# Seven block products for eight contraction tiles in two output projections

## The chip, the cores and the metric

The kernel runs on one core of a Trainium2 chip. Its time is the device time of one execution in microseconds (us). A core has five engines that run their own instruction lists and wait for each other by semaphores: TensorE (PE in the profile; PEld is its weight load), VectorE (DVE), ScalarE (ACT), GpSimd (POOL) and SyncE (SP), which here issues DMA transfers. Matmuls write into PSUM, a small memory of eight banks; all else lies in SBUF.

## The reference

The program is a trunk of two layers on a sequence of T = 512 tokens and D = 1024 channels in float32. Each layer has a sequence mixer (a state-space mixer in the first, a spatial gating mixer in the second) and a channel mixer, each followed by a layer norm of `sqrt(2) * x + y`. The channel mixer is what the change touches:

```
def conv_ffn(x, w_in, conv_w, conv_b, w_out):      # x: 512 x 1024
    h = causal_dwconv(x @ w_in, conv_w, conv_b)    # 512 x 5632, 3 taps along the tokens
    g, u = split(h, 2)                             # 512 x 2816 each
    return (silu(g) * u) @ w_out                   # (512 x 2816) @ (2816 x 1024)
...
x = layer_norm(sqrt(2) * x + conv_ffn(x, ...))
```

The contraction of the output projection has 2816 = 22 x 128 channels, so 22 tiles.

## The kernel before

*Split float32.* A product of two float32 matrices is done as three products of rounded parts. Each operand `a` is split into `hi` (a cast by ACT to the matmul's float32 format) and `lo = a - hi` (a subtraction by DVE), and PE adds up `hi*hi + hi*lo + lo*hi` in one PSUM bank. So each 128x128 by 128x512 block costs three matmuls.

*Weights.* All weights lie in DRAM as a list of 250 tiles of 128x1024 (`wall`). `w_prep` (lines 74 to 84) goes through that list: SP loads a tile into one of three raw buffers (L78), ACT casts it (L80), DVE subtracts (L82). `hi` and `lo` have seven buffers each, and `w_get(i)` has tiles up to i + 6 prepared before it hands out tile i.

*Channel mixer.* `ffn` (from line 542) runs 22 steps; step j multiplies two weight tiles with the layer's transposed input (`xT_hi`, `xT_lo`: 8 x 512 columns each, kept in split form), convolves both results on ACT and DVE (L178, L180) and stores `silu(gate) * up` as `h[:, j, :]`, 128 channels by 512 tokens (L565). In step 1 `affine_res` applies the last norm's scale and bias to the residual `xres` (L309, L310).

*Output projection.* `out_proj` (from line 205) takes all eight PSUM banks as an accumulator `acc[t][h]`: four row blocks of 128 tokens by two halves of 512 columns. For each contraction tile k it gets the split activation tile (`Split.get`, L192 and L193, six buffers), the split weight tile, and does 4 x 2 x 3 = 24 matmuls (L214 to L216). The last four or five tiles are done row block by row block, so that `stats` (L252 on) can add the residual (L259), do the norm's statistics and scale while PE is at the next row block. POOL does `(var + eps) ** -0.5` there on 128x1 elements (L203).

*Order.* The program is written as tiles and operations in one text. A scheduler gives each engine its list from planned times and the order of the text; the lists are then run in order, and an instruction whose semaphore isn't there holds up all that stand behind it on its engine.

Of the kernel before, what the change touches and what calls it, by code (L numbers as in the profile page):

```python
# [14 lines left out]
P = 128  # L15
T = 512
# [33 lines left out]
LOOK = 6  # L50


@with_exitstack
def trunk_kernel(ctx, tc, x_tok, x_t, w_dt, wall, pp, ln_g, ln_b, b_v, b_s, w_s_t, out):
# [17 lines left out]
    wnext = [0]  # L72

    def w_prep(upto):
        while wnext[0] <= min(upto, W_ALL - 1):
            i = wnext[0]
            raw = wpool.tile([P, 1024], F32, tag="wraw", bufs=3, name=f"wraw{i}")
            nc.sync.dma_start(raw, wall[i])  # L78
            hi = wpool.tile([P, 1024], F32R, tag="whi", bufs=WB, name=f"whi{i}")
            nc.scalar.copy(hi, raw)  # L80
            lo = wpool.tile([P, 1024], F32R, tag="wlo", bufs=WB, name=f"wlo{i}")
            nc.vector.tensor_sub(lo, raw, hi.bitcast(F32))  # L82
            wready[i] = (hi, lo)
            wnext[0] += 1

    def w_get(i, look=LOOK):
        w_prep(i + look)
        return wready.pop(i)
# [3 lines left out]
    xT_hi = const.tile([P, NK, T], F32R, name="xT_hi")  # L92
    xT_lo = const.tile([P, NK, T], F32R, name="xT_lo")
# [29 lines left out]
    def mm_k(o, w, k, lo, hi):  # L123
        whi, wlo = w
        cs = slice(k * P, (k + 1) * P)
        nc.tensor.matmul(o, whi[:, cs], xT_hi[:, k, lo:hi], start=(k == 0), stop=False)  # L126
        nc.tensor.matmul(o, whi[:, cs], xT_lo[:, k, lo:hi], start=False, stop=False)  # L127
        nc.tensor.matmul(o, wlo[:, cs], xT_hi[:, k, lo:hi], start=False, stop=(k == NK - 1))  # L128

    with tc.tile_pool(name="xload", bufs=8) as xl:  # L130
        wdt = xl.tile([P, NK, 32], F32, name="wdt", bufs=1)
        xr = []
        for q in range(4):
            for k in (2 * q, 2 * q + 1):
                xr.append(xl.tile([P, T], F32, tag="xr", name=f"xr{k}"))
                nc.sync.dma_start(xr[k], x_t[:, k, :])
                nc.scalar.copy(xT_hi[:, k, :], xr[k])
                nc.vector.tensor_sub(xT_lo[:, k, :], xr[k], xT_hi[:, k, :].bitcast(F32))
# [44 lines left out]
    class Split:  # L183
# [4 lines left out]
        def pre(self, k, tag=""):  # L188
            bufs = self.bufs if not tag else 1
            hi = self.pl.tile([P, T], F32R, tag="ahi" + tag, bufs=bufs, name=f"ahi{self.base}_{k}")  # L190
            lo = self.pl.tile([P, T], F32R, tag="alo" + tag, bufs=bufs, name=f"alo{self.base}_{k}")
            nc.scalar.copy(hi, self.act(k))  # L192
            nc.vector.tensor_sub(lo, self.act(k), hi.bitcast(F32))  # L193
            self.done[k] = (hi, lo)
# [10 lines left out]
    def out_proj(lnp, split, base, nk, ln, last, hooks=None, nxt=None, mid=None):  # L205
        if last:
            gb, bb = ln_bc(lnp, base, ln)
        acc = [[pst(f"acc{base}_{t}_{h}") for h in range(2)] for t in range(NT)]

        def mm(t, h, k, a, w):  # L210
            o = acc[t][h]
            ts_ = slice(t * P, (t + 1) * P)
            hs = slice(h * T, (h + 1) * T)
            nc.tensor.matmul(o, a[0][:, ts_], w[0][:, hs], start=(k == 0), stop=False)  # L214
            nc.tensor.matmul(o, a[0][:, ts_], w[1][:, hs], start=False, stop=False)  # L215
            nc.tensor.matmul(o, a[1][:, ts_], w[0][:, hs], start=False, stop=(k == nk - 1))  # L216

        k0 = 0
        if hooks is not None:
# [32 lines left out]
        def stats(t):  # L252
            r = lnp.tile([P, D], F32, tag="r", bufs=2, name=f"r{base}_{t}")
# [21 lines left out]
        def trans(t):  # L275
            for h in range(2):
# [9 lines left out]
                xh = xT_hi[:, 4 * h:4 * h + 4, t * P:(t + 1) * P]  # L286
                nc.scalar.copy(xh, xf)
                nc.vector.tensor_sub(xT_lo[:, 4 * h:4 * h + 4, t * P:(t + 1) * P], xf, xh.bitcast(F32))
# [10 lines left out]
    def ln_bc(pl, base, ln):  # L299
        gb = pl.tile([P, D], F32, name=f"lng{base}")  # L300
        bb = pl.tile([P, D], F32, name=f"lnb{base}")
# [242 lines left out]
    def ffn(ip, base_o, li, ln, last, nxt=None):  # L544
        with ExitStack() as st:
# [3 lines left out]
            split = Split(sp, base_o, lambda k: h[:, k, :])  # L549
# [17 lines left out]
            out_proj(lnp, split, base_o, 22, ln, last, nxt=nxt)  # L567


    def v_tile(cb, t, ws):  # L570
        ps = pst(f"pv{cb}_{t}")
        ts_ = slice(t * P, (t + 1) * P)
        for k in range(NK):
            whi = ws[k // 2][0][:, (k % 2) * T:(k % 2) * T + T]
            wlo = ws[k // 2][1][:, (k % 2) * T:(k % 2) * T + T]
            nc.tensor.matmul(ps, xT_hi[:, k, ts_], whi, start=(k == 0), stop=False)  # L576
            nc.tensor.matmul(ps, xT_hi[:, k, ts_], wlo, start=False, stop=False)  # L577
            nc.tensor.matmul(ps, xT_lo[:, k, ts_], whi, start=False, stop=(k == NK - 1))  # L578
# [98 lines left out]
def _pack(i):  # L677
# [27 lines left out]
    wall = np.concatenate(tiles, 0)  # L705

# [54 lines left out]
```

## Time and profile before

| | us |
|---|---|
| median of 3 runs | 1439.64 |
| lowest, highest | 1439.13, 1439.78 |
| the profiled execution | 1439.39 |
| its span, first to last instruction | 1437.5 |
| PE busy | 1423.6 (99%) |
| DVE busy | 846.1 (59%) |
| ACT busy | 611.5 (43%) |
| POOL busy | 23.7 (2%) |

The profile is one execution. It has the busy time of each engine, the span in 40 equal slices with the clock that TensorE was granted, the chain of work that ended last, the costliest groups of instructions, and each instruction with its start. A matmul's listed duration overlaps that of the next; the distance of their starts is what each costs.

### The profile page before, as it was taken

Reading aid. Unit: us, or ns where it says so; the run is one execution under the profiler, and the core shown is the slowest. Engines: PE = TensorE matmul, PEld = TensorE weight load, DVE = VectorE, ACT = ScalarE, POOL = GpSimd, SP = SyncE. Lnnn points to the kernel's source line nnn. Section 1 sums busy time; section 2 is a strip of 40 time slices with the busy share of each in tenths; the row PEclk is TensorE's granted clock in tenths of the full one; section 3 lists DMA queues with packets and bytes.
Section 4 is the critical chain, followed back from the end, with each engine's and each line's share of the span. In section 5 each row is a group of like instructions: output and inputs, shape, how many; then the busy total and the mean of one; then the engine's idle time right before and its main releaser. Section 6 shows DMA issues by size and latency. Waiting matters only on the chain.

```text
span 1437.5 us, 17317 instructions
## 1 busy us (share of the span) xinstructions
PE 1423.6 (99%) x6911; PEld 1187.8 (83%) x6911; DVE 846.1 (59%) x1147; ACT 611.5 (43%) x893; POOL 23.7 (2%) x30
## 2 busy tenths in 40 slices
PE   8999999999999999999999999999999999999997
PEld 6788888888889888888888888888888888888886
DVE  6878777565378655554336556446378655554336
ACT  5886677343245433333233433223255433333220
POOL 0000000000000000000000000000000000000001
PEclk9999999999999999999999999999999999999999
DMA  6533322333424332323331432223223333333311
GB/s 219 206 106 129 106 100 74 88 115 122 160 73 123 112 99 92 103 90 101 93 98 59 154 125 88 88 88 118 89 81 127 101 103 93 98 103 118 103 44 59
DMA packets 42864, 152.66 MB, mean 106 GB/s; under 512 B 4760, under 2 KB 6040, under 8 KB 41504
## 3 DMA queue, kind: packets, MB, share of 16 engines
q1 hardware_dynamic: 40240, 143.17, 31.0%
q10 hardware_dynamic: 2544, 8.39, 1.7%
q8 instruction: 54, 0.88, 0.2%
q14 instruction: 26, 0.21, 0.0%
HBM read 149.37 MB, written 2.18 MB: 105 GB/s over the span
## 4 chain that ended last, share of the span: by engine, by line
PE 96%; ACT 1%; DVE 1%; DMA 1%; issue 0%; SPq 0%; DVEq 0%; ACTq 0%
PE ip L126 18%; PE ip L127 18%; PE ip L128 18%; PE acc L216 10%; PE acc L214 10%; PE acc L215 10%; PE pv L576 2%; PE pv L578 2%; PE pv L577 2%; PE psp L636 1%; PE py L443 1%; PE pt L279 1%; PE po L450 1%; PE pst L429 1%; PE pcb L384 0%; PE px L395 0%
## 5 line engine op out<-in xcount | busy, mean ns | idle before, releaser
L126 PE MATMUL ip<-xT_hi,whi 128*128 128x512 f32 (+1 forms) x1264 | 484.4, 383 | 0.0
L128 PE MATMUL ip<-xT_hi,wlo 128*128 128x512 f32 (+1 forms) x1264 | 479.8, 380 | 0.0
L127 PE MATMUL ip<-xT_lo,whi 128*128 128x512 f32 (+1 forms) x1264 | 478.7, 379 | 0.0
L82 DVE TENSOR_TENSOR wlo<-wraw,whi 128x1024 fp32r<-128x1024 f32 x242 | 295.7, 1223 | 297.8 <-ACT whi L80 297.3
L80 ACT CAST whi<-wraw 128x1024 fp32r<-128x1024 f32 x242 | 253.8, 1051 | 355.8 <-PE ip L127 289.3
L126 PEld LDWEIGHTS ip<-xT_hi,whi 128*128 128x128 f32 x1264 | 237.9, 188 | 45.3 <-issue 1.2
L128 PEld LDWEIGHTS ip<-xT_hi,wlo 128*128 128x128 f32 x1264 | 237.7, 188 | 44.6
L127 PEld LDWEIGHTS ip<-xT_lo,whi 128*128 128x128 f32 x1264 | 238.0, 188 | 43.3 <-issue 0.2
L214 PE MATMUL acc<-whi,ahi 128*128 128x512 f32 x608 | 237.3, 390 | 0.0
L216 PE MATMUL acc<-whi,alo 128*128 128x512 f32 x608 | 236.6, 389 | 0.0
L215 PE MATMUL acc<-wlo,ahi 128*128 128x512 f32 x608 | 236.5, 389 | 0.0
L214 PEld LDWEIGHTS acc<-whi,ahi 128*128 128x128 f32 x608 | 114.1, 188 | 24.2 <-issue 0.8
L216 PEld LDWEIGHTS acc<-whi,alo 128*128 128x128 f32 x608 | 114.1, 188 | 23.7
L215 PEld LDWEIGHTS acc<-wlo,ahi 128*128 128x128 f32 x608 | 114.1, 188 | 23.6
L193 DVE TENSOR_TENSOR alo<-h,ahi 128x512 fp32r<-128x512 f32 x44 | 30.4, 691 | 103.4 <-ACT ahi L192 103.4
L192 ACT CAST ahi<-h 128x512 fp32r<-128x512 f32 x44 | 27.4, 623 | 141.7 <-PE acc L215 119.5
L180 DVE SCALAR_TENSOR_TENSOR cv<-ip,ppt,cv 128x511 f32<-128x511 f32 (+2 forms) x90 | 66.9, 744 | 2.0 <-ACT cv L178 1.9
L180 DVE SCALAR_TENSOR_TENSOR gt<-ip,ppt,gt 128x511 f32<-128x511 f32 x88 | 65.7, 746 | 1.6 <-ACT gt L178 0.3
L180 DVE SCALAR_TENSOR_TENSOR ut<-ip,ppt,ut 128x511 f32<-128x511 f32 x88 | 65.7, 746 | 1.3
L563 ACT ACTIVATE gt<-gt 128x512 f32<-128x512 f32 x44 | 27.8, 632 | 82.6 <-DVE gt L180 82.5
L284 ACT ACTIVATE xf<-pt,ppt 128x128 f32<-128x128 f32 x96 | 36.6, 466 | 46.0 <-PE pt L279 43.6
L576 PE MATMUL pv<-whi,xT_hi 128*128 128x512 f32 x128 | 50.0, 390 | 0.0
(138 smaller groups left out, 1073.9 us busy)
## 6 DMA issues: line engine op xcount, KB each, us to landing
wraw<-in_wall_dram SPq DMA_DIRECT2D x242, 512.0 KB
xres<-scr SPq DMA_DIRECT2D x8, 1024.0 KB
xr<-in_x_t_dram SPq DMA_DIRECT2D x8, 256.0 KB
xres<-rscr SPq DMA_DIRECT2D x2, 1024.0 KB
xres<-in_x_tok_dram ACTq DMA_DIRECT2D x1, 2048.0 KB
out_dram<-r SPq DMA_DIRECT2D x8, 256.0 KB
wraw_s<-in_wall_dram SPq DMA_DIRECT2D x8, 128.0 KB
lngf<-in_ln_g_dram ACTq DMA_DIRECT2D x2, 512.0 KB
```

The lines of the kernel that those rows point to most:

```text
L80: nc.scalar.copy(hi, raw)
L82: nc.vector.tensor_sub(lo, raw, hi.bitcast(F32))
L126: nc.tensor.matmul(o, whi[:, cs], xT_hi[:, k, lo:hi], start=(k == 0), stop=False)
L127: nc.tensor.matmul(o, whi[:, cs], xT_lo[:, k, lo:hi], start=False, stop=False)
L128: nc.tensor.matmul(o, wlo[:, cs], xT_hi[:, k, lo:hi], start=False, stop=(k == NK - 1))
L180: nc.vector.scalar_tensor_tensor(o[:, s:], ps[:, :T - s], col(c + taps - 1 - s), o[:, s:], ALU.mult, ALU.add)
L193: nc.vector.tensor_sub(lo, self.act(k), hi.bitcast(F32))
L214: nc.tensor.matmul(o, a[0][:, ts_], w[0][:, hs], start=(k == 0), stop=False)
L215: nc.tensor.matmul(o, a[0][:, ts_], w[1][:, hs], start=False, stop=False)
L216: nc.tensor.matmul(o, a[1][:, ts_], w[0][:, hs], start=False, stop=(k == nk - 1))
L284: nc.scalar.activation(xf[:, q, :], pt[:, q * P:(q + 1) * P], AF.Identity, scale=col(c), bias=col(c + 8))
L576: nc.tensor.matmul(ps, xT_hi[:, k, ts_], whi, start=(k == 0), stop=False)
```

## The change

The first eight contraction tiles of the two channel mixers' output projections are a product of a 512x1024 matrix A and a 1024x1024 matrix B. Both are cut into four quarters: A11, A12 (the first 256 tokens, contraction tiles 0 to 3 and 4 to 7), A21, A22 (the other 256 tokens), B11 to B22 likewise (contraction by columns). Winograd's form of Strassen's scheme gets the product from seven products of quarters in place of eight:

- activation sums S1 = A21 - A22, S4 = A12 - (A11 - S1), S3 = A21 - A11 (written over A21), S2 = A11 - S1. All on POOL, each 128 partitions by 4 x 256 elements; three of the operations from step 10 of the 22 on, S2 inside the projection.
- weight sums T1 = B11 + B12, T2 = B11 + B22, T3 = B22 + B12, T4 = T2 + B21, in halves of 128x1024: eight POOL additions per layer. The host's packing orders the quarters anew, without adding any up.
- the products in the order A11 B11, S4 B22, A12 B21, S1 T1, S2 T2, S3 T3, A22 T4. Each is two row blocks by four contraction tiles by three matmuls.

The weight sums need all four quarters at once. Their raw loads, eight of 512 KB, go into the space of `xT_hi` and `xT_lo`, which is free once the input projection has done its last matmul; B11, B22 and B21 are also loaded on their own, as before, for the first three products. What goes to several quarters of the result is added into `xres` by DVE from PSUM, in place of part of the residual sum. Two buffers for the norm's scale and bias move from one pool to another so that the sums can share their space. The other 14 tiles are as before. The core of the diff:

```diff
+SEVEN = (W_F1O, W_F2O)
+QUARTER = ("11", "22", "21", "12")
...
+    def w_sum(b, n, s):
+        if n == "T1" and s == 0:
+            c_new(b)
+        slots = [v[:, 2 * m:2 * m + 2, :].rearrange("p a b -> p (a b)") for v in craw for m in range(4)]
+        at = dict(zip(("11", "12", "22", "21"), range(4)))
+        if n == "T1" and s == 0:
+            for q in ("11", "12"), ("22", "21"):
+                for m in range(2):
+                    for e in q:
+                        nc.sync.dma_start(slots[2 * at[e] + m], wall[b + 2 * QUARTER.index(e) + m])
+        r11, r12, r22, r21 = (slots[2 * m + s] for m in range(4))
+        o, x, y = {"T1": (r11, r11, r12), "T2": (r11, r11, r22), "T3": (r12, r22, r12), "T4": (r21, r11, r21)}[n]
+        nc.gpsimd.tensor_tensor(o, x, y, ALU.add)
+        return o
...
+            i = wseq[wnext[0]]
+            if isinstance(i, tuple):
+                raw = w_sum(*i)
...
+        def prod(o, a, w, first):
+            for i in range(2):
+                for k in range(4):
+                    ah, al = (v[:, (k % 2) * 256 + i * P:(k % 2) * 256 + (i + 1) * P] for v in a[k // 2])
+                    wh, wl = (v[:, (k % 2) * T:(k % 2) * T + T] for v in w[k // 2])
+                    nc.tensor.matmul(o[i], ah, wh, start=(first and k == 0), stop=False, skip_group_check=True)
+                    nc.tensor.matmul(o[i], ah, wl, start=False, stop=False, skip_group_check=True)
+                    nc.tensor.matmul(o[i], al, wh, start=False, stop=(k == 3), skip_group_check=True)
+
+        def seven():
+            qa, qc, qd, qb = ([acc[2 * m][h], acc[2 * m + 1][h]] for m in range(2) for h in range(2))
...
+            prod(qa, *operands("A11", base, base + 1), True)
+            for i in range(2):
+                for m, h, op in ((0, 1, ALU.subtract), (1, 0, ALU.add), (1, 1, ALU.subtract)):
+                    v = xres[:, 2 * m + i, h * T:(h + 1) * T]
+                    nc.vector.scalar_tensor_tensor(v, v, ALPHA, qa[i], ALU.mult, op)
+            prod(qc, *operands("S4", base + 2, base + 3), True)
+            sums()
+            prod(qa, *operands("A12", base + 4, base + 5), False)
+            prod(qb, *operands("S1", *two("T1")), True)
+            for i in range(2):
+                v = xres[:, 2 + i, 0:T]
+                nc.vector.tensor_add(v, v, qb[i])
+            prod(qb, *operands("S2", *two("T2")), False)
+            for i in range(2):
+                v = xres[:, i, T:]
+                nc.vector.tensor_add(v, v, qb[i])
+            prod(qb, *operands("S3", *two("T3")), False)
+            for i in range(2):
+                v = xres[:, 2 + i, 0:T]
+                nc.vector.tensor_sub(v, v, qb[i])
+            prod(qd, *operands("A22", *two("T4")), True)
+            if not last:
+                x_new(base)
...
-                nc.vector.scalar_tensor_tensor(r[:, hs], xres[:, t, hs], ALPHA, acc[t][h], ALU.mult, ALU.add)
+                if sums is not None and (t > 1 or h):
+                    nc.vector.tensor_add(r[:, hs], xres[:, t, hs], acc[t][h])
+                else:
+                    nc.vector.scalar_tensor_tensor(r[:, hs], xres[:, t, hs], ALPHA, acc[t][h], ALU.mult, ALU.add)
...
+            def less(o, a, b):
+                nc.gpsimd.tensor_tensor(o, a, b, ALU.subtract)
+
+            def sums_first():
+                less(tsum("S1", "lng"), quarter("21"), quarter("22"))
+                less(tsum("S4", "lnb"), quarter("11"), tmp["S1"])
+                less(tmp["S4"], quarter("12"), tmp["S4"])
+                tmp["S3"] = quarter("21")
+                less(tmp["S3"], quarter("21"), quarter("11"))
+
+            def sums_then():
+                less(tsum("S2", "lnb"), quarter("11"), tmp["S1"])
...
-                        affine_res(fp, f"f{li}", ln - 1)
+                        affine_res(sp, f"f{li}", ln - 1)
+                    if j == 10:
+                        sums_first()
                     if j == 21:
-                        for kk in range(2):
-                            split.pre(kk)
+                        for m in range(2):
+                            split.pre(("A11", m))
```

## Rows read from the trace of the kernel before

**Rows 1.** The page: busy time and share, granted clock by slice, shares of the chain.
```profile
PE 1423.6 (99%) x6911; PEld 1187.8 (83%) x6911; DVE 846.1 (59%) x1147; ACT 611.5 (43%) x893; POOL 23.7 (2%) x30
...
PEclk9999999999999999999999999999999999999999
...
PE 96%; ACT 1%; DVE 1%; DMA 1%; issue 0%; SPq 0%; DVEq 0%; ACTq 0%
```

**Rows 2.** Timeline (start, duration), PE, first matmuls of tiles 0 and 1.
```profile
665.11 0.39 PE L214 MATMUL acc<-whi,ahi 128*128 128x512 f32 x1
...
670.55 0.39 PE L214 MATMUL acc<-whi,ahi 128*128 128x512 f32 x1
```

**Rows 3.** Busy time by stretch: start:end, length, busy us of each engine, clock, DMA.
```profile
665.10:703.20 38.10, 38.10 (x170) 31.54 (x169) 14.84 (x16) 11.19 (x15) 0.00 (x0) 1.00 0.31 97
```

**Rows 4.** Groups by line: busy us, mean ns of one, idle before.
```profile
L82 DVE TENSOR_TENSOR wlo<-wraw,whi 128x1024 fp32r<-128x1024 f32 x242 | 295.7, 1223 | 297.8 <-ACT whi L80 297.3
L80 ACT CAST whi<-wraw 128x1024 fp32r<-128x1024 f32 x242 | 253.8, 1051 | 355.8 <-PE ip L127 289.3
...
L193 DVE TENSOR_TENSOR alo<-h,ahi 128x512 fp32r<-128x512 f32 x44 | 30.4, 691 | 103.4 <-ACT ahi L192 103.4
L192 ACT CAST ahi<-h 128x512 fp32r<-128x512 f32 x44 | 27.4, 623 | 141.7 <-PE acc L215 119.5
...
L259 DVE SCALAR_TENSOR_TENSOR r<-xres,acc 128x512 f32<-128x512 f32 x32 | 21.7, 684 | 20.8 <-PE acc L216 20.8
```

**Rows 5.** Timeline, ACT, first activation split of the first output projection.
```profile
448.94 0.62 ACT L192 CAST ahi<-h 128x512 fp32r<-128x512 f32 x1 [0.47 <-DVE h L565]
```

**Rows 6.** Timeline, SP and ACT: weight loads, their casts, and the last norm's load.
```profile
454.35 3.86 SPq L78 DMA_DIRECT2D wraw<-in_wall_dram  x3
...
457.78 1.05 ACT L80 CAST whi<-wraw 128x1024 fp32r<-128x1024 f32 x1 [0.45 <-DMA wraw<-in_wall_dram]
...
460.45 1.06 ACT L80 CAST whi<-wraw 128x1024 fp32r<-128x1024 f32 x1 [0.94 <-DMA wraw<-in_wall_dram]
...
462.52 1.05 ACT L80 CAST whi<-wraw 128x1024 fp32r<-128x1024 f32 x1 [0.48 <-DMA wraw<-in_wall_dram]
...
1314.68 0.33 ACTq L302 DMA_DIRECT2D lng<-in_ln_g_dram  x1
```

**Rows 7.** Busy time by stretch, two with much DMA (last column GB/s).
```profile
8.00:12.00 4.00, 3.88 (x8) 2.77 (x9) 3.82 (x8) 3.60 (x9) 0.00 (x0) 1.00 1.01 367
...
458.00:462.00 4.00, 4.00 (x19) 3.32 (x18) 3.33 (x5) 3.06 (x4) 0.00 (x0) 1.00 0.88 264
```

**Rows 8.** Timeline, POOL: its longest operations.
```profile
338.86 2.91 POOL L492 TENSOR_TENSOR small<-small 128x16 f32<-128x16 f32 x1 [39.24 <-DVE small L491]
...
805.80 1.10 POOL L607 TENSOR_SCALAR_AFFINE_SELECT wsr<-wsr 128x1024 f32<-128x1024 f32 x1 [13.52 <-DMA wsr<-in_w_s_t_dram]
```

**Rows 9.** Timeline, POOL: the norms' power on 128x1 elements.
```profile
406.63 0.55 POOL L203 TENSOR_TENSOR rs<-rs,small 128x1 f32<-128x1 f32 x1 [64.87 <-DVE rs L202]
...
426.87 1.39 POOL L203 TENSOR_TENSOR rs<-rs,small 128x1 f32<-128x1 f32 x1 [7.92 <-DVE rs L202]
...
872.91 1.40 POOL L203 TENSOR_TENSOR vrs<-vrs,small 128x1 f32<-128x1 f32 x1 [4.96 <-DVE vrs L202]
...
1071.92 1.39 POOL L203 TENSOR_TENSOR rs<-rs,small 128x1 f32<-128x1 f32 x1 [7.92 <-DVE rs L202]
1411.55 0.98 POOL L203 TENSOR_TENSOR rs<-rs,small 128x1 f32<-128x1 f32 x1 [338.24 <-DVE rs L202]
...
1425.21 0.91 POOL L203 TENSOR_TENSOR rs<-rs,small 128x1 f32<-128x1 f32 x1 [5.88 <-DVE rs L202]
```

**Rows 10.** Timeline, DVE beside three of these.
```profile
426.64 1.22 DVE L82 TENSOR_TENSOR wlo<-wraw,whi 128x1024 fp32r<-128x1024 f32 x1
...
872.69 1.23 DVE L82 TENSOR_TENSOR wlo<-wraw,whi 128x1024 fp32r<-128x1024 f32 x1
...
1411.39 1.41 DVE L266 SCALAR_TENSOR_TENSOR r<-r,mv,lng 128x512 f32<-128x512 f32 x2
```

More of the change, by code (lines that the diff above doesn't have):

```diff
@@ L86, in w_get @@
     def w_get(i, look=LOOK):
-        w_prep(i + look)
+        w_prep(wpos[i] + look)
         return wready.pop(i)
@@ L189, in pre @@
             bufs = self.bufs if not tag else 1
[L190 to L193, printed above, removed]
+            nm = "_".join(map(str, k)) if isinstance(k, tuple) else k
+            hi = self.pl.tile([P, T], F32R, tag="ahi" + tag, bufs=bufs, name=f"ahi{self.base}_{nm}")
+            lo = self.pl.tile([P, T], F32R, tag="alo" + tag, bufs=bufs, name=f"alo{self.base}_{nm}")
+            a = self.act(k)
+            h3, l3 = hi, lo
+            if len(a.shape) == 3:
+                h3, l3 = (v.rearrange("p (a b) -> p a b", b=a.shape[2]) for v in (hi, lo))
+            nc.scalar.copy(h3, a)
+            nc.vector.tensor_sub(l3, a, h3.bitcast(F32))
             self.done[k] = (hi, lo)
@@ L203, in rstd_of, with out_proj @@
         nc.gpsimd.tensor_tensor(out2[:, 1:2], out2[:, 0:1], nhalf[:, 0:1], ALU.pow)
-    def out_proj(lnp, split, base, nk, ln, last, hooks=None, nxt=None, mid=None):
+    def out_proj(lnp, split, base, nk, ln, last, hooks=None, nxt=None, mid=None, sums=None, rpool=None):
         if last:
@@ L208, in out_proj @@
         acc = [[pst(f"acc{base}_{t}_{h}") for h in range(2)] for t in range(NT)]
+        more = sums is not None
         def mm(t, h, k, a, w):
@@ new lines, in mm @@
+            nc.tensor.matmul(o, a[1][:, ts_], w[0][:, hs], start=False, stop=(k == nk - 1), skip_group_check=more)
+        def prod(o, a, w, first):
[6 more added lines that the diff above has]
+                    nc.tensor.matmul(o[i], al, wh, start=False, stop=(k == 3), skip_group_check=True)
@@ new lines, in seven, with operands, two @@
+        def seven():
+            qa, qc, qd, qb = ([acc[2 * m][h], acc[2 * m + 1][h]] for m in range(2) for h in range(2))
+            def operands(n, *ws):
+                w = [w_get(x, LOOK - m) for m, x in enumerate(ws)]
+                return [split.get((n, m)) for m in range(2)], w
+            def two(n):
+                return [(base, n, s) for s in range(2)]
+            prod(qa, *operands("A11", base, base + 1), True)
[21 more added lines that the diff above has]
+                x_new(base)
@@ L218, in out_proj @@
         k0 = 0
-        if hooks is not None:
+        if sums is not None:
+            seven()
+            k0 = 8
+        elif hooks is not None:
             k0 = 3
@@ L548, in ffn, with quarter, act, tsum @@
             sp = pool(st, f"sp{li}")
-            split = Split(sp, base_o, lambda k: h[:, k, :])
+            tmp = {}
+            def quarter(n):
+                r, c = (4 * (int(v) - 1) for v in n)
+                return h[:, c:c + 4, 64 * r:64 * r + 256]
+            def act(k):
+                if not isinstance(k, tuple):
+                    return h[:, k, :]
+                n, m = k
+                v = tmp[n] if n in tmp else quarter(n[1:])
+                return v[:, 2 * m:2 * m + 2, :]
+            def tsum(n, tag):
+                tmp[n] = sp.tile([P, D], F32, tag=tag, bufs=1, name=f"{n}_{li}").rearrange("p (k t) -> p k t", k=4)
+                return tmp[n]
+            def less(o, a, b):
[8 more added lines that the diff above has]
+                less(tsum("S2", "lnb"), quarter("11"), tmp["S1"])
+            split = Split(sp, base_o, act)
             with ExitStack() as st2:
@@ L566, in ffn @@
             lnp = pool(st, f"lnp{li}")
-            out_proj(lnp, split, base_o, 22, ln, last, nxt=nxt)
+            out_proj(lnp, split, base_o, 22, ln, last, nxt=nxt, sums=sums_then, rpool=sp)
     def v_tile(cb, t, ws):
@@ L705, in _pack @@
     wall = np.concatenate(tiles, 0)
+    for b in SEVEN:
+        w4 = wall[b:b + 8].reshape(2, 2, 2, P, 2, T)
+        wall[b:b + 8] = np.stack(
+            [w4[int(q[0]) - 1, s, :, :, int(q[1]) - 1, :].transpose(1, 0, 2).reshape(P, 1024)
+             for q in QUARTER for s in range(2)])
     pp = np.zeros((P, C_ALL), np.float32)
```

67 lines of the change are left out of this document (43 added, 24 removed).

## The prediction

> **What bounds the kernel now.** The page's first part comes first: PE is busy for 99% of the span, DVE for 59%, ACT for 43%, POOL for 2%, and the chain that ended last is 96% PE [rows 1]. The granted clock is 9 or more in all 40 slices [rows 1], so it is at the upper of its two levels (2.4 GHz) throughout. Next the stretch that is edited: PE in order of time at the head of the first mixer's output projection. The first matmul of contraction tile 0 starts at 665.11, the first of tile 1 at 670.55 [rows 2]; that is 24 matmuls in 5.44 us, 0.227 us each, without a gap (the 0.39 us beside each is its pipelined length). Eight tiles take 43.5 us there. In the window that the new products would fill, DVE is busy 14.8 of 38.1 us, ACT 11.2, POOL 0 [rows 3]. So the time is PE's count of matmuls as long as DVE, ACT and POOL deliver operands, and the question is whether they still do.
>
> **What goes.** Eight tiles are 8 x 24 = 192 matmuls. Seven products of 2 (row blocks) x 4 (contraction tiles) x 3 = 24 matmuls are 168. The shape of each stays 128x128 by 128x512. 24 fewer in each of two projections: 2 x 24 x 0.227 = 10.9 us less, and no more is to be had.
>
> **What comes, and where it lies.** I count t from the projection's first matmul (665.11; the second layer likewise). The products start at t = 0 (A11), 5.4 (S4), 10.9 (A12), 16.3 (S1), 21.8 (S2), 27.2 (S3), 32.6 (A22), end 38.1.
> - Splits. 14 weight operands are split instead of 8, and 14 activation operands instead of 8: six more casts of 1.05 and six of 0.62 us on ACT, six more subtractions of 1.22 and six of 0.69 us on DVE [rows 4] per layer. ACT gains 10 us and goes from 11.2 to about 21 of 38: hidden. DVE gains 11.5.
> - PSUM updates. Six fused operations after A11 and six additions after S1, S2 and S3 read PSUM; the nearest row is the residual sum, 0.68 us [rows 4]: 8.2 us more on DVE. DVE's load becomes 14.8 + 11.5 + 8.2 = 34.5 of 38 us. It fits, barely, if nothing else stops DVE. The A11 reads have a whole product (S4) before PE overwrites that bank, the S1 and S2 reads of the second row block have 2.7 us.
> - Order. Each engine's list is not the program's text order: the cast of activation tile 0, written at step j = 21, runs at 448.94 [rows 5], more than 200 us ahead. So a late weight sum doesn't block all that is written behind it; the first six activation splits (A11, S4, A12) and six weight splits will be done before t = 0, and the three products that need no weight sum cost nothing. What is queued is queued by planned times, and if the real times are longer, what stands behind waits.
> - Weight loads. Eight 512 KB loads go into the input's buffers, so SP can issue them only when PE has read these for the last time, at t = 0; two raw loads of the old kind go away. A load's issue at 454.35 leads to its cast at 457.78, 3.4 us; the ones behind it come 2.0 to 2.7 us apart [rows 6]. The DMA moved 264 to 367 GB/s where it was busiest [rows 7], so 1.4 to 2.0 us for 512 KB. I take 5.5 us for the first pair, 1.65 for each further load: the pairs are there at t = 5.5, 8.8, 12.1, 15.4. SP's later loads stand behind them; three are already in their buffers, so nobody waits.
> - Weight sums. Eight POOL additions of 128x1024 per layer. No row shows one. From below: a one-operand pass of the same tile took 1.10 us [rows 8]. From above: POOL's longest two-operand row, 2.9 us [rows 8]. I take two passes, 2.2 us. The Trainium skill (GPSIMD Engine Reference, Elementwise) has 4497 ns for twice the length, which would make it 2.25 us; no run here shows it.
> - Activation sums: five POOL subtractions per layer during the input projection, where PSUM's ring of eight banks and the six-deep weight buffer stand between DVE and PE. No cost. The same for the biases moved to another pool and the sums of the statistics (an addition instead of a fused one, 0.69 against 0.68 us). Tail after the last matmul: unchanged.
>
> **The shared read side.** Without any conflict every sum is in time: T1's first half is added at 5.5 to 7.7, cast and subtracted by 10.1, wanted at 16.3; all eight additions back to back from 5.5 end by 23.1 or soon after the last pair, T4's second half is ready at about 26, wanted at 34. But POOL and DVE don't run freely beside each other. POOL's 128x1 power took 0.55 us where DVE did nothing, and 1.39 to 1.40 us in the four cases (three shown) where it began inside a weight subtraction of DVE [rows 9, 10]: begun 426.87, DVE's subtraction ended 427.86, POOL's end 428.26; begun 872.91, DVE's end 873.92, POOL's 874.31. Each time POOL ends 0.40 us after DVE. In the last stage it took 0.91 to 0.98 (four cases, two shown) beside a fused DVE operation with two SBUF operands [rows 9, 10]. So an operation of POOL that reads SBUF waits out a DVE operation with two SBUF operands. That DVE waits out POOL's, no row shows, since POOL has no long one. Bounds: DVE waits for nothing, or for a whole addition of 2.2 us. I take the latter, as the exclusion seen goes by whole instructions, and keep both. The Trainium skill (SBUF — State Buffer, Who interferes with whom) states the same conflict, and that whichever issued first holds the shared ports for its whole instruction. The first half agrees with the 1.39 us rows; by the second half the sum is the one below, without it the first rival.
>
> If additions and two-operand subtractions go one after another, what stands ahead of product S2's first matmul is, in order of the inputs' arrival: six additions (T1, T2 and T3; T3 needs only loads, so it is not planned behind T2's wait for T1's subtractions) 6 x 2.2 = 13.2; six weight subtractions 7.3; four activation subtractions (S1, S2, S3) 2.8; two casts of 1.05 in which neither side can go on, 2.1. That is 25.4 us from t = 5.5: t = 30.9, where PE wants it at 21.8. 9.1 us late, against 5.4 saved: 3.7 us lost per layer, 7.3 in both. The reads of S1's sum stand in the same DVE list, so the wait will show as one stall at S2. Least: with the best order, four additions, four weight and three activation subtractions ahead of S2 (15.8 + 2.1, 1.6 us late), then the other four additions and what goes with them (15.8 again) ahead of A22's second half, 3.6 late: 5.2 per layer, nothing lost or won. Most: T4's two additions and subtractions also stand ahead, 6.8 more: 15.9 late, 10.5 lost, 21 in all.
>
> **The sum.** The profiled execution took 1439.39 us at a span of 1437.5, 0.25 below the median of 1439.64. 1439.4 - 10.9 + 18.2 = 1446.7, so 1447.
>
> **The rivals.**
> 1. DVE isn't held up by POOL. For it: no row shows DVE waiting, and the additions are spread over 25 us. POOL still waits for DVE: about 0.6 us for each of eight additions, up to 5 us on a slack of 4.5 to 8, which costs 0 to 3 us per layer. The result is 1439.4 - 10.9 = 1428.5 to 1434.5, middle 1430.5: faster. It decides from 5.4 us of stall per layer: below that the change wins. Against it: the exclusion in [rows 9, 10] is by whole instructions. Chance 0.32.
> 2. The exclusion is there but the order is near the best, or an addition is near 1.1 us (eight then take 8.8 instead of 17.6 us): stall and saving cancel, 1437 to 1442. For it: lists are made by planned time [rows 5]. Chance 0.10.
> 3. The loads are the limit: at 264 GB/s, and in the second layer 1 MB of scale and bias sent at 1314.68 [rows 6] among them, the last pair lands 4 to 7 us later than taken. Without exclusion that eats the slack and costs 1 to 3 us per layer: 1431 to 1435. Against: 367 GB/s was seen [rows 7]. Chance 0.05.
>
> **How the numbers follow.** Forecast (a stall at S2 longer than the saving) 0.53: its own range is 1442 to 1460. What a measurement of this kernel can tell from no change is 0.2%, 2.9 us. Faster 0.32 + 0.05 = 0.37, same 0.10, slower 0.53. The range for 8 in 10 has to hold the first rival too, as it has a third of the chance: from 1429.5 (its lowest us left out) to 1457.
>
> **What would show it.** PE: 48 matmuls fewer, intervals still 0.227 us within a product. If the forecast holds, PE stands idle once per output projection, 7 to 13 us, before S2, released by DVE; POOL's additions show 2.2 us or more with starts at DVE's ends, and DVE's subtractions in that stretch are spread out or longer than 1.22 us. If rival 1 holds, DVE's subtractions start while additions run and PE has gaps under 3 us. If rival 3, the first waits of POOL are for DMA until late. If the additions take under 1.5 us or over 3, the terms of the sum are wrong with the mechanism right; over 3 us, even rival 1 would lose. A stall at S4 or A12 would mean that the order of the lists was misjudged.

## The result, and the profile after

The changed kernel took 1461.03 us (median of 4, 1459.51 to 1463.13) against 1439.68 us for the kernel before beside it (1439.13 to 1439.78): a ratio of 1.0150 [1.0133, 1.0168] (95% interval). The forecast was 1447, with a range of 1429.5 to 1457. The sign and the mechanism came out, the size didn't.

The page of the changed kernel, the lines that answer to [rows 1]: busy time and share of each engine, granted clock by slice, and the chain that ended last.

```profile
PE 1416.5 (97%) x6863; PEld 1181.2 (81%) x6863; DVE 910.5 (62%) x1195; ACT 627.3 (43%) x917; POOL 95.4 (7%) x56
...
PEclk9999999999999999999899999999999999999899
...
PE 89%; ACT 3%; POOL 2%; DVE 2%; DMA 2%; issue 1%; SPq 0%; DVEq 0%; POOLq 0%; ACTq 0%
```

The 48 matmuls are gone (6911 to 6863), and PE's busy time fell by 7.1 us where the working had 10.9 (some matmuls became slower, as the clock below shows). The span rose from 1437.5 to 1457.8 us, so PE now stands idle for 41.3 us, not 13.9. The chain is no longer nearly all PE, and two slices of the clock show an 8: both hold an output projection.

PE's waits, summed over the run (what waited, for whom: total us, times, longest):

```profile
PE acc L270 <- DVE xres L295: 23.5, 2, 11.8
...
PE acc L271 <- DVE wlo_T L112: 2.9, 2, 2.0
```

L295 is DVE's addition of product S1's PSUM bank to the residual; PE may start S2 in that bank only behind it. That is one stall per layer, at S2 and released by DVE, as forecast, with a small one inside S1 ahead of it. The first layer in order of time, PE (start, duration; in brackets the idle time before, and its releaser). t = 0 of the prediction, the first matmul of the projection, is 664.67 here.

```profile
680.99 0.39 PE L270 MATMUL acc<-whi_T,ahi_S 128*128 128x512 f32 x1
...
683.62 0.50 PE L271 MATMUL acc<-wlo_T,ahi_S 128*128 128x512 f32 x1 [0.88 <-DVE wlo_T L112]
...
699.52 0.76 PE L270 MATMUL acc<-whi_T,ahi_S 128*128 128x512 f32 x1 [11.72 <-DVE xres L295]
700.08 0.63 PE L271 MATMUL acc<-wlo_T,ahi_S 128*128 128x512 f32 x1
700.51 0.63 PE L272 MATMUL acc<-whi_T,alo_S 128*128 128x512 f32 x1
...
704.23 0.40 PE L272 MATMUL acc<-whi_T,alo_S 128*128 128x512 f32 x1
```

S1 starts at t = 16.3, on time. S2 starts at t = 34.9, where it was wanted at 21.8 (in the second layer at 36.0, 1355.64 less 1319.62). Then comes something that the prediction had no term for: the matmuls behind the stall are 0.43 us apart, not 0.227. Eleven of them, from 699.52 to 704.23, take 4.71 us where 11 x 0.227 is 2.50. The stretches say why (start:end, length, busy us of PE, PEld, DVE, ACT, POOL, granted clock, DMA share, GB/s); these answer to [rows 3].

```profile
687.80:699.50 11.70, 0.01 (x1) 0.01 (x1) 8.39 (x7) 7.60 (x10) 6.41 (x3) 0.61 0.00 0
699.50:701.50 2.00, 1.98 (x5) 1.61 (x6) 2.00 (x4) 0.26 (x1) 0.00 (x0) 0.50 0.00 0
701.50:703.50 2.00, 2.00 (x7) 1.52 (x6) 1.95 (x2) 0.00 (x0) 0.00 (x0) 0.50 0.00 0
703.50:705.50 2.00, 2.00 (x9) 1.64 (x8) 0.84 (x2) 0.00 (x0) 0.00 (x0) 0.85 0.49 100
705.50:707.50 2.00, 2.00 (x11) 1.63 (x10) 1.75 (x4) 1.68 (x3) 0.00 (x0) 1.00 0.40 162
```

While PE idles the granted clock falls to 0.50 (1.2 GHz, the lower of its two levels), and PE has been at work again for some 4 us when it is back at 1.00. In the second layer the wait is 11.76 us, and nine matmuls from 1355.64 take 3.90 instead of 2.04 us.

So the rows give nearly the whole bill: waits 23.5 + 2.9 = 26.4; half clock 2.2 + 1.9 = 4.1; saved 10.9; 26.4 + 4.1 - 10.9 = 19.6, where the span grew by 20.3. The other 0.7 us isn't traced.

What DVE was behind with shows in its list and POOL's. POOL's eight weight additions, the rows that were missing before:

```profile
671.12 2.40 POOL L96 TENSOR_TENSOR cr_hi<-cr_hi 128x1024 f32<-128x1024 f32 x1 [138.80 <-DMA cr_hi<-in_wall_dram]
673.60 2.74 POOL L96 TENSOR_TENSOR cr_hi<-cr_lo,cr_hi 128x1024 f32<-128x1024 f32 x1
676.29 3.38 POOL L96 TENSOR_TENSOR cr_hi<-cr_hi 128x1024 f32<-128x1024 f32 x1
...
682.55 3.26 POOL L96 TENSOR_TENSOR cr_lo<-cr_hi,cr_lo 128x1024 f32<-128x1024 f32 x1
...
691.94 2.35 POOL L96 TENSOR_TENSOR cr_lo<-cr_hi,cr_lo 128x1024 f32<-128x1024 f32 x1
```

And DVE beside them, which answers to [rows 4] and [rows 10] (x2, x3: so many in a row):

```profile
670.31 1.88 DVE L288 SCALAR_TENSOR_TENSOR xres<-xres,acc 128x512 f32<-128x512 f32 x3
...
674.64 2.78 DVE L112 TENSOR_TENSOR wlo_T<-cr_hi,whi_T 128x1024 fp32r<-128x1024 f32 x1 [0.57 <-ACT whi_T L110]
...
680.79 6.11 DVE L112 TENSOR_TENSOR wlo_T<-cr_hi,whi_T 128x1024 fp32r<-128x1024 f32 x2 [0.57 <-ACT whi_T L110]
686.82 2.85 DVE L238 TENSOR_TENSOR alo_S<-S,ahi_S 128x512 fp32r<-128x512 f32 x1
692.98 4.67 DVE L112 TENSOR_TENSOR wlo_T<-cr_hi,whi_T 128x1024 fp32r<-128x1024 f32 x3 [3.31 <-ACT whi_T L110]
697.57 1.21 DVE L112 TENSOR_TENSOR wlo_T<-cr_lo,whi_T 128x1024 fp32r<-128x1024 f32 x1
698.70 0.68 DVE L295 TENSOR_TENSOR xres<-xres,acc 128x512 f32<-128x512 f32 x1
```

An addition takes 2.35 to 2.40 us when it begins with no subtraction of DVE under way (the first and the last), and up to 3.38 when one is. A subtraction of DVE that took 1.22 takes 2.78 when it begins inside an addition, one of 0.69 takes 2.85: its listed time now holds its waiting. The addition from 673.60 ended at 676.34, the subtraction begun inside it 1.08 us later, about its time alone. The next addition, begun at 676.29, ended 2.25 us after that. So the two engines take turns by whole instructions, from 672 to 694.3. DVE's updates with one operand in SBUF and the other in PSUM (L288) aren't held up: three took 1.88 us, the last of them beside the first addition. And the read of S1's sum, which PE waits for, is the last in this row: ahead of it in DVE's list stands the subtraction of T4's first half (697.57), an operand of the last product, wanted 11 us later.

### The profile page after: what moved, and what is told of

It is laid out like the page before. It is cut to its first block, busy times and chain, and to the rows that moved or that the text cites. A ratio compares the mean times of both kernels' runs of the same rounds, so it can differ in the third digit from the quotient of the medians.

```text
span 1457.8 us, 17353 instructions
## 1 busy us (share of the span) xinstructions
PE 1416.5 (97%) x6863; PEld 1181.2 (81%) x6863; DVE 910.5 (62%) x1195; ACT 627.3 (43%) x917; POOL 95.4 (7%) x56
## 4 chain that ended last, share of the span: by engine, by line
PE 89%; ACT 3%; POOL 2%; DVE 2%; DMA 2%; issue 1%; SPq 0%; DVEq 0%; POOLq 0%; ACTq 0%
PE ip L166 18%; PE ip L167 18%; PE ip L168 18%; PE acc L261 7%; PE acc L263 7%; PE acc L262 7%; POOL cr_hi L96 2%; PE pv L709 2%; PE pv L707 2%; PE pv L708 2%; PE psp L767 1%; PE py L542 1%; PE acc L270 1%; PE acc L271 1%; PE acc L272 1%
## 5 line engine op out<-in xcount | busy, mean ns | idle before, releaser
L112 DVE TENSOR_TENSOR wlo<-wraw,whi 128x1024 fp32r<-128x1024 f32 x238 | 291.4, 1226 | 273.9 <-ACT whi L110 273.2
L110 ACT CAST whi<-wraw 128x1024 fp32r<-128x1024 f32 x238 | 249.4, 1051 | 336.5 <-PE ip L167 272.6
L261 PE MATMUL acc<-whi,ahi 128*128 128x512 f32 x480 | 187.5, 391 | 0.0
L263 PE MATMUL acc<-whi,alo 128*128 128x512 f32 x480 | 186.8, 389 | 0.0
L262 PE MATMUL acc<-wlo,ahi 128*128 128x512 f32 x480 | 186.8, 389 | 0.0
L261 PEld LDWEIGHTS acc<-whi,ahi 128*128 128x128 f32 x480 | 90.1, 188 | 19.3 <-issue 0.8
L263 PEld LDWEIGHTS acc<-whi,alo 128*128 128x128 f32 x480 | 90.1, 188 | 18.7
L262 PEld LDWEIGHTS acc<-wlo,ahi 128*128 128x128 f32 x480 | 90.1, 188 | 18.5
L237 ACT CAST ahi<-h 128x512 fp32r<-128x512 f32 x28 | 17.4, 621 | 83.0 <-PE acc L262 45.9
L238 DVE TENSOR_TENSOR alo<-h,ahi 128x512 fp32r<-128x512 f32 x28 | 19.3, 691 | 54.0 <-ACT ahi L237 54.0
```

## The experiments

The theory after the result: (1) POOL and DVE exclude each other by whole instructions, because both read SBUF; (2) DVE's list makes it worse, because it puts work for the late products ahead of a read that PE waits for; (3) the idle time is billed once more through the clock. Rivals: the sums come too late in any form; DVE is simply full; the order alone is at fault. All medians in us, of four executions (ten for e3, five for e11); the kernel before ran beside them at 1439.53 (the first four), 1439.69 (the next four) and 1440.47 (the last two).

| run | median (lowest to highest) | ratio to before, 95% interval |
|---|---|---|
| e1_no_sums | 1429.45 (1427.80 to 1430.32) | 0.9922 [0.9906, 0.9939] |
| e2_write_only | 1433.06 (1431.07 to 1434.90) | 0.9951 [0.9936, 0.9966] |
| e3_dve_sums | 1439.82 (1437.91 to 1442.68) | 1.0002 [0.9993, 1.0012] |
| e4_pool_order | 1459.75 (1458.96 to 1460.62) | 1.0137 [1.0121, 1.0152] |
| e5_dma_sums | 1467.37 (1467.05 to 1467.86) | 1.0192 [1.0175, 1.0209] |
| e6_pool_order2 | 1451.30 (1449.93 to 1452.64) | 1.0081 [1.0066, 1.0096] |
| e8_dve_order | 1431.70 (1430.37 to 1432.77) | 0.9944 [0.9929, 0.9959] |
| e9_fill_gap | 1457.36 (1456.71 to 1459.98) | 1.0126 [1.0111, 1.0141] |
| e10_one_operand | 1454.67 (1453.40 to 1456.27) | 1.0101 [1.0087, 1.0115] |
| e11_dve_order2 | 1428.79 (1428.20 to 1430.81) | 0.9923 [0.9910, 0.9937] |

**e1_no_sums: leave the weight additions out.**

```
-        nc.gpsimd.tensor_tensor(o, x, y, ALU.add)
```

> The eight weight additions per layer are left out: T1 to T4 are split straight from one raw quarter each. Loads, splits, activation sums, products and PSUM updates stay. Theory (POOL's additions and DVE's two-operand operations exclude each other, and what stands behind in DVE's list waits): no gap of PE over 1 us in the output projections, 1428.5 to 1431 us. Rival 'loads or DVE's own load are the limit': the gap before S2 stays at 5 us or more per layer, 1439 us or more.

1429.45, 10.1 under the kernel before. The whole saving is there as soon as the additions are gone, and PE is busy without a gap through the projection (38.50 of 38.50 us from 664.5 to 703). So loads, splits, updates from PSUM and the activation sums cost nothing; the 31.6 us to the changed kernel hang on eight additions per layer.

**e2_write_only: POOL as busy, but not reading.**

```
-        nc.gpsimd.tensor_tensor(o, x, y, ALU.add)
+        nc.gpsimd.memset(o, 0.0)
+        nc.gpsimd.memset(o, 0.0)
+        nc.gpsimd.memset(o[:, 0:512], 0.0)
```

> Each POOL addition becomes three fills of the same tile (whole, whole, half), which write SBUF and read nothing; the sums are left out. By the fills of the trace (0.20 us for 128 columns, 0.10 for one) they keep POOL busy about 2.3 us in place of each addition. Theory (it is the reading that excludes): DVE's weight subtractions take 1.22 us again, no stall above 1 us, 1428.5 to 1431 us. Rival 'POOL is too slow by itself': T2's second half is still done 7th, after some 17 us of POOL, and the gap before S2 is 3 us or more per layer, 1434 us or more.

1433.06, 2 us over the top of what was expected, and far from the changed kernel. POOL and DVE, timeline:

```profile
670.29 0.96 POOL L97 MEMSET cr_hi<- 128x1024 f32 x1
671.19 0.96 POOL L96 MEMSET cr_hi<- 128x1024 f32 x1
672.09 0.53 POOL L98 MEMSET cr_hi<- 128x512 f32 x1
...
673.73 1.23 DVE L114 TENSOR_TENSOR wlo_T<-cr_hi,whi_T 128x1024 fp32r<-128x1024 f32 x1 [1.03 <-ACT whi_T L112]
```

POOL works back to back from 669.28 to 687.7, 2.3 us in place of each addition (24 fills in 18.4 us), and DVE's subtraction is at 1.23 us inside it. It begins 1.8 us earlier than in the changed kernel, since a fill waits for one landed block and not for two; that is little beside a stall of 11.7. So it is neither POOL being busy, nor its writing, nor the 2.3 us by which each operand comes later. What is left over e1 are two waits of 1.1 and 1.4 us for a cast of A22's activations.

**e3_dve_sums: the additions on DVE.**

```
-        nc.gpsimd.tensor_tensor(o, x, y, ALU.add)
+        nc.vector.tensor_tensor(o, x, y, ALU.add)
```

> The same additions on DVE, complete result. Theory: an addition costs 1.22 us on DVE as the 128x1024 ones of before do, nothing excludes anything; in DVE's list some 7 additions (8.5), 7 weight subtractions (8.5) and 1.4 us of others stand between the first landing (t = 6.4) and the read of S1's PSUM, so it comes at t = 25 to 26 in place of 19, and S2 starts 3 to 4 us late: 1434 to 1438 us. Rival 'DVE has no room for it' (34.5 + 9.8 of 38 us): 6 us late or more per layer, 1441 us or more.

1439.82, about 2 over the top of the expected range, and 21.2 better than the changed kernel with DVE given 19.5 us more to do. DVE is busy without a break (start:end, length, busy PE, PEld, DVE, ...):

```profile
686.40:690.00 3.60, 2.32 (x8) 1.19 (x8) 3.60 (x5) 0.65 (x2) 0.00 (x0) 1.00 0.00 0
690.00:694.00 4.00, 3.00 (x14) 2.21 (x13) 4.00 (x5) 2.00 (x2) 0.00 (x0) 1.00 0.00 0
```

PE's waits in the products of sums are 0.3, 1.1 and 1.0 us in the first layer and 4.1 us in the second; the last of the first layer and that of the second are for the `lo` part of S2's activations, which stands in DVE's list behind T4's addition and subtraction. Behind the 4.1 us wait the granted clock is again 0.50, for 12 matmuls.

**e4_pool_order: POOL's additions in the order of the products,** T1, T1, T2, T2 and so on (in the changed kernel the order was T1, T3, T1, T2, T4, T3, T2, T4 by halves).

```
...
+            with tc.issue_after(prev[0]):
+                prev[0] = nc.gpsimd.tensor_tensor(o, x, y, ALU.add).ins
```

> Only the order of POOL's additions changes: T1, T1, T2, T2, T3, T3, T4, T4, where T2's second half was 7th. Complete result. Theory: the read of S1's PSUM still stands behind the subtraction of T4's first half in DVE's list, and so behind the 7th addition: gap 11 to 14 us per layer, 1458 to 1463 us. Rival 'the late T2 is the cause': T2 is there three additions (7 to 10 us) earlier, gap 3 to 6 us, 1440 to 1447 us.

1459.75. PE still waits 13.1 and 13.7 us at S2 for the read of S1's sum:

```profile
699.98 0.77 PE L276 MATMUL acc<-whi_T,ahi_S 128*128 128x512 f32 x1 [13.12 <-DVE xres L301]
...
1355.46 0.76 PE L276 MATMUL acc<-whi_T,ahi_S 128*128 128x512 f32 x1 [13.70 <-DVE xres L301]
```

DVE ahead of that read:

```profile
686.65 9.30 DVE L118 TENSOR_TENSOR wlo_T<-cr_hi,whi_T 128x1024 fp32r<-128x1024 f32 x3 [0.57 <-ACT whi_T L116]
695.98 3.25 DVE L118 TENSOR_TENSOR wlo_T<-cr_lo,whi_T 128x1024 fp32r<-128x1024 f32 x1
699.16 0.68 DVE L301 TENSOR_TENSOR xres<-xres,acc 128x512 f32<-128x512 f32 x1
```

So POOL's order by itself isn't the cause. T3's subtractions and T4's first (of cr_lo, 3.25 us) still stand ahead of the read in DVE's list, so the read still comes behind seven additions.

**e5_dma_sums: the sums by accumulating transfers.** What its transfers left in the buffers isn't the sums, so only their time is read.

```
+        nc.sync.dma_start(o, wall[b + 2 * QUARTER.index(first) + s])
+        for e in more:
+            nc.gpsimd.dma_start(o, wall[b + 2 * QUARTER.index(e) + s], accum_op=ALU.add)
-        nc.gpsimd.tensor_tensor(o, x, y, ALU.add)
```

> The changed kernel, but each summed weight half is formed by the transfers: the first block is loaded, the second (for T4 also the third) is added to it in SBUF by an accumulating transfer. No engine adds; 18 transfers of 512 KB per layer instead of 8; the result is complete. Theory (the loss is the reading of two SBUF operands by GpSimd and VectorE at the same time): GpSimd's 2.4 us additions are gone, so VectorE's subtractions of the summed weights are back at 1.22 us. If accumulating transfers move at the loads' rate (1.65 to 2.0 us per 512 KB) T4 is there at about t = 33, and the time is 1428.5 to 1434; if at half that rate T4 is about 13 us late and the time is 1445 or more, with TensorE waiting at S3 and A22, not at S2. Rival (the loss comes from the summed weights being late in any form, whoever adds): a stall at S2 as in the changed kernel, 1455 or more.

1467.37, the slowest. ACT's casts of T1's two halves and of T4's first:

```profile
682.56 1.04 ACT L106 CAST whi_T<-cr_hi 128x1024 fp32r<-128x1024 f32 x1 [11.87 <-DMA cr_hi<-in_wall_dram]
686.33 1.04 ACT L106 CAST whi_T<-cr_hi 128x1024 fp32r<-128x1024 f32 x1 [2.21 <-DMA cr_hi<-in_wall_dram]
...
702.55 1.04 ACT L106 CAST whi_T<-cr_lo 128x1024 fp32r<-128x1024 f32 x1 [6.93 <-DMA cr_lo<-in_wall_dram]
```

The first half of T1 is cast at t = 18 (in the changed kernel at 673.56, t = 9), T4's first half at 38. PE waits already at S1, and at both row blocks of S2: 10.7 us in the first layer. The expectation of waits at S3 and A22 and none at S2 was wrong: an accumulating transfer took 10.5 to 15.3 us from issue to landing (median by buffer). DVE's subtractions are at 1.22 to 1.23 us here, with POOL not adding: that part holds. The time is also what the rival of late sums forecast (1455 or more), so this run decides nothing between the two: here the transfers make the sums late. e2 above and e8 below speak against that rival for the changed kernel.

**e6_pool_order2: additions on POOL, DVE's list mended.** The splits of T3 are queued behind the first read of S1's sum, those of T4 behind the first read of S2's, and the activation splits of the next product ahead of both.

```
+            def later(x, n):
+                cap[0] = wpos[(base, n, 1)]
+                with tc.issue_after(x.ins):
+                    w_prep(cap[0])
...
-                nc.vector.tensor_add(v, v, qb[i])
+                x = nc.vector.tensor_add(v, v, qb[i])
+                if i == 0:
+                    later(x, "T3")
...
```

> The changed kernel with GpSimd's additions in text order and with VectorE's list mended: the activation splits of S2, S3 and A22 stand ahead, T3's subtractions stand behind the first read of S1's PSUM, T4's behind the first read of S2's. The result is complete. Two parts of the loss are told apart: the exclusion itself (additions 8 x 2.4, weight subtractions 8 x 1.22, activation subtractions some 7 x 0.69 one after another from t = 6.4 give 40 or more where A22's second half is wanted at 34) and the queueing behind the wrong instruction (VectorE's read of S1's sum behind T4's first half). Theory: both count; the list mended gives back the smaller part: 5 to 9 us of stall per layer stay, partly at S2 and partly at S3 and A22, each shorter than in the changed kernel: 1439 to 1449. If queueing is all of it: 1429 to 1433. If the list is not the matter: 1457 to 1461, one stall of 12 us at S2 as before.

1451.30, 2.3 over the top. The waits went from 11.7 and 11.8 to 8.7 and 9.4 us, and stayed at S2:

```profile
690.71 4.95 DVE L246 TENSOR_TENSOR alo_S<-h,ahi_S 128x512 fp32r<-128x512 f32 x2 [0.54 <-ACT ahi_S L245]
695.59 0.67 DVE L314 TENSOR_TENSOR xres<-xres,acc 128x512 f32<-128x512 f32 x1
```

Two subtractions of 0.69 us take 4.95 us here: each has to let an addition pass. Five additions must come ahead of the read by the lists (ACT casts T3's first half before S3's activations), but POOL runs on into the sixth and seventh while DVE waits its turn. So both parts are real: of the 31.6 us between the changed kernel and e1 the list is worth 9.7 while the additions are on POOL, and 21.9 stay. These hold the exclusion, the lower clock behind the stall and what order may be left; the next run says more of their size.

**e8_dve_order: additions on DVE, the same mended list** (e3's edit and e6's list; POOL has no additions left to order).

> The weight additions on VectorE (1.22 us each) and the same mended list: activation splits ahead, T3's additions and subtractions behind the first read of S1's sum, T4's behind the first read of S2's. The result is complete. Theory: nothing excludes VectorE any more, and what was left in the run with the additions on VectorE alone (1439.8, waits of 1 to 4 us at S2 for an activation subtraction that stood behind T4's) was queueing: by the list T3's halves are ready at t = 26 (wanted 27.2) and T4's at 32.5 (wanted 32.6), so 0 to 1.5 us of waits per layer: 1428.5 to 1432. Rival (VectorE is simply full: 14.8 + 11.5 + 8.2 + 9.8 = 44 us of work in 38): 1436 to 1440 in whatever order.

1431.70: 8.0 under the kernel before and 8.1 under e3, which does the same work. So DVE wasn't full: 8.1 us of e3 were queueing. Against e6, which has the same list, it is 19.6 us less: that is what having the additions on POOL cost there, with the turns, their greater length and the clock together. What remains is a wait of 0.3 and 1.0 us for the first read of S2's sum.

**e9_fill_gap: keep PE at work in the wait.**

```
+            w = s1[1][1][0]
+            for _ in range(44):
+                nc.tensor.matmul(qd[0], w[:, 0:P], w[:, 0:T], start=True, stop=True, skip_group_check=True)
```

> The changed kernel with 44 more matmuls of the same shape (44 x 0.227 = 10.0 us) put behind product S1; they read S1's weights, write the PSUM bank that A22 starts anew later, and their results are not used. They lie in the 11.7 us in which TensorE waited before S2. Theory (behind the idle stretch TensorE runs at a granted clock of 0.50, matmuls of 0.43 us, for some 10 matmuls or 2.6 us per layer): the wait shrinks to about 2 us, S2 starts at the same moment, its matmuls take 0.227 us from the first, and the time falls by up to 5 us though 88 matmuls are added: 1455 to 1458. Rival (the slow matmuls behind the stall have another cause, late operands or contention): no change, 1460 to 1463, the intervals behind the stall still 0.4 us.

1457.36, 3.7 under the changed kernel though it does 88 matmuls more; the mean granted clock of its four executions was 0.996 to 0.999, of the changed kernel's 0.987 to 0.991. PE in the profiled execution, which was the slowest of the four at 1459.98:

```profile
688.19 10.13 PE L296 MATMUL acc<-whi_T 128*128 128x512 f32 x44
...
700.26 0.47 PE L270 MATMUL acc<-whi_T,ahi_S 128*128 128x512 f32 x1 [1.93 <-DVE xres L299]
...
702.23 0.63 PE L270 MATMUL acc<-whi_T,ahi_S 128*128 128x512 f32 x1
```

Here the clock still fell, 0.9 us after S2 began, for some eight matmuls: 1.5 us lost instead of 2.2, and 1.7 instead of 1.9 in the second layer. So in this execution, whose time is about that of the changed kernel's profiled one (1459.51), the filler gave back 0.9 us of clock; that the three others, at 1456.7 to 1457.8, lost less or nothing can be read from their mean clock alone. The two ratio intervals overlap a little, 1.0111 to 1.0141 and 1.0133 to 1.0168. The clock term itself stands on the rows of the changed kernel; that keeping PE busy avoids it is made likely here, and not shown to its full size.

**e10_one_operand: POOL reads one operand, not two.** Two copies in place of each addition; the sums are left out.

```
-        nc.gpsimd.tensor_tensor(o, x, y, ALU.add)
+        nc.gpsimd.tensor_copy(o, y)
+        nc.gpsimd.tensor_copy(o, y)
```

> The changed kernel with each of GpSimd's eight weight additions per layer replaced by two copies of one operand into the same buffer (128x1024 each); the sums are left out, the split and everything behind it stay. A copy should be near the 1.10 us of GpSimd's one-operand pass in the kernel before, so GpSimd is busy nearly as long (16 x 1.1 = 17.6 us per layer against 19.2) but reads one SBUF operand, not two. Theory A (what excludes VectorE is an operation of GpSimd that reads two SBUF operands): VectorE's subtractions of the summed weights take 1.22 us again, no wait at S2 over 1.5 us, 1429 to 1434. Theory B (any reading by GpSimd excludes VectorE's two-operand operations): subtractions of 2.3 us and more, since GpSimd's two copies let VectorE in between them, and a stall at S2 of 6 to 12 us per layer, 1444 to 1460.

1454.67: by the time and by the wait theory B. POOL, then DVE:

```profile
671.32 1.05 POOL L97 COPY cr_hi<-cr_hi 128x1024 f32<-128x1024 f32 x1
672.43 1.38 POOL L96 COPY cr_hi<-cr_hi 128x1024 f32<-128x1024 f32 x1
673.87 1.92 POOL L97 COPY cr_hi<-cr_hi 128x1024 f32<-128x1024 f32 x1
...
674.81 2.96 DVE L239 TENSOR_TENSOR alo_S<-S,ahi_S 128x512 fp32r<-128x512 f32 x2
...
680.78 3.90 DVE L113 TENSOR_TENSOR wlo_T<-cr_hi,whi_T 128x1024 fp32r<-128x1024 f32 x2 [3.01 <-ACT whi_T L111]
```

A copy of 1.04 to 1.05 us stretches to 1.38, 1.92 and 2.03 beside DVE, DVE's pair of 0.69 us subtractions to 2.96 and its pair of 1.22 to 3.90. That is 1.95 a subtraction, not the 2.3 and more of theory B: a copy is shorter than an addition, so the turn comes sooner. So POOL's copies take turns with DVE's two-operand operations as its additions do; with e2, which only writes, the read side is shown from both ends. The size isn't comparable in full, since in this build one matmul of A22 came ahead of S2 in PE's list and PE waited 8.1 us for its operand. The Trainium skill (SBUF — State Buffer, Who interferes with whom) says the same: a VectorE operation with two SBUF inputs contends with a GpSimd one that reads SBUF, not with one that only writes. The traces agree, at 1.23 us beside memsets and 2.78 beside an addition.

**e11_dve_order2: one step more.** A22's two activation subtractions behind the reads of S2's sum.

```
-            for m in range(2):
-                split.pre(("A22", m))
...
+            with tc.issue_after(x.ins):
+                for m in range(2):
+                    split.pre(("A22", m))
```

> The version with the additions on VectorE and the mended list, with one thing moved: the two activation subtractions of A22 stand behind the second read of S2's sum and T4's subtractions, not ahead of the first read. There the first read of S2's sum was late by 0.3 us in the first layer and 1.0 in the second. The result is complete. Theory: that wait goes, and A22's second operand is there at t = 33.3, wanted at 33.0, so up to 0.7 us comes back per layer: 1430 to 1432, 0 to 1 us under the version before it, at most 2 us above the run without any sums (1429.5). Rival (VectorE's last places are full and any order gives a wait somewhere): 1432 to 1434.

1428.79, 1.2 us under the range expected, 0.8% under the kernel before and 2.2% under the changed one; it computes all of the reference. The projection of the first layer:

```profile
664.50:703.00 38.50, 38.50 (x172) 31.87 (x171) 35.49 (x43) 19.45 (x25) 0.00 (x0) 1.00 0.34 126
```

PE is busy for all 38.50 us, DVE for 35.49. That is all that seven products can save (10.9 worked out; 1440.47 - 1428.79 = 11.7 measured, 9.1 to 13.0 by the interval): eight additions per layer cost nothing on the engine that seemed too full for them.

## Why the prediction was wrong, point by point

- *The bound, and what goes.* Right: 48 matmuls, 0.227 us each, and the whole 10.9 us shows once nothing stalls (e1, e11).
- *Splits, PSUM updates, loads, activation sums at nothing.* Right; e1 and e11 hold all of them. The first addition began at t = 6.5, the estimate was 5.5. POOL waited for a transfer only at the first addition. Rival 3 is out.
- *DVE waits out POOL's additions whole (rival 1 says it doesn't).* Right: 2.78 us where 1.22 is alone. Rival 1's 1428.5 to 1434.5 is the time of a kernel without the exclusion, and e2, at 1433.06, is such a kernel.
- *One stall at S2, released by DVE, the read of S1's sum in the same list.* Right in place and in releaser, but for 0.9 and 2.0 us inside S1 that weren't forecast. Rival 2 is out.
- **The step that failed** is the term "six additions (T1, T2 and T3 ...) 6 x 2.2 = 13.2". An addition was 2.35 to 2.40 us by itself, not 2.2, and not six but all eight had run before S2 began. T4's first half is wanted last, but it needs only loads and T2, so POOL did it fifth and DVE's subtraction for it stood ahead of the read; the other half was POOL running on while DVE waited. Eight additions from t = 6.5 ended at 29.6, the last subtractions and the read came behind them, and S2 began at 34.9: 13.1 us late, not 9.1. The text's "Most" case, with T4 ahead, was 15.9 late. I gave the order of inputs' arrival for T3 and trusted that T4 would keep its place, with nothing in the trace to say so. e6 holds the check: there T4's subtractions stand behind the read, and S2 begins at t = 30.6 and 31.5, where the forecast had 30.9. That it fits so well is partly luck, since T3's subtractions stand behind the read as well and seven additions had begun.
- **A term that was missing**: what an idle stretch costs behind it. The trace of before had no long wait of PE in the middle of its work, and its clock column is at 9 in every slice; the stall was priced by its length alone. The rows add 2.2 and 1.9 us; e9 took back 0.9 of these by its rows, and its median is 3.7 lower. But the trace of before did hold a price, at the start of the program, behind 4.71 us in which PE had nothing to do:

```profile
4.71 0.80 PE L126 MATMUL ps_b<-xT_hi,whi_s 128*128 128x512 f32 x1 [4.71 <-ACT whi_s L111]
...
10.29 0.63 PE L127 MATMUL ps_b<-xT_lo,whi_s 128*128 128x512 f32 x1
10.72 0.63 PE L128 MATMUL ps_b<-xT_hi,wlo_s 128*128 128x512 f32 x1
```

These matmuls are 0.43 us apart with 0.63 listed, as behind the stall where the clock column has 0.50; the column has 1.00 for them (8 to 12 us in [rows 7]). So the reading of [rows 1] as full clock throughout was wrong for the first 13 us, and the distance of matmuls is the safer sign.

- *The sum.* Per layer 9.1 - 5.4 = 3.7 was forecast. Measured: 12.6 and 13.8 of waiting, 2.2 and 1.9 of half clock, so 14.8 and 15.7 in all; less 5.4 each, 9.4 and 10.3 us were lost per layer.

Open: why the accumulating transfers took 10 us and more each, what decides whether the clock falls, and how much of e10's 8.1 us is the exclusion and how much PE's order.

## What to carry to other kernels

Work given to GpSimd isn't free because GpSimd is idle: if it reads SBUF while VectorE does operations on two SBUF operands, the two take turns. Here 1.22 us for an addition on VectorE itself beat 2.40 us on GpSimd beside it, by 21.2 us in all (e3 against the changed kernel). What decides is not an engine's busy share but what stands in its list ahead of the one instruction that the bounding engine waits for; 8 us came from the order alone with the same operations (e3 to e8). And a wait of the bounding engine should be priced at its length and, if it is of this size, some 2 us for the lower clock behind it.

## What the runs showed of the hardware

- GpSimd with 128x1024 float32: an addition of two SBUF operands 2.35 to 2.40 us, a copy 1.04, a memset 0.96; VectorE's addition 1.22 (e3). For the addition the Trainium skill (GPSIMD Engine Reference, Elementwise) has 4497 ns at twice the length, an estimate of 2.25 us; the run gives 2.40.
- GpSimd's one-operand copies exclude VectorE's two-operand operations as its additions do (e10); memsets don't (e2). VectorE's additions of an SBUF and a PSUM operand kept their time beside a GpSimd addition (1.88 us for three in the changed kernel, the last one beside it; two in e6).
- The profile puts the waiting for the shared read side into the instruction's own duration, so no wait is listed: in the changed kernel the 12 subtractions of T1 to T3 have a mean of 2.38 us, where 1.22 is work.
- The granted clock fell to 0.50 in or behind waits of PE of 11.7, 8.7, 8.1 and 4.1 us (changed kernel, e6, e10, e3), but in e9 also behind one of 1.9, while behind 2.05 us inside S1 of the changed kernel's second layer it stayed at 1.00, as behind those of 0.3 to 1.4 us in e2 and e8. So the length of the one wait doesn't settle it, and what does isn't shown here.
